# Five of thirteen weight slots moved by 32 bytes, and the down-projection tail of the second feed-forward moved from those five to the other eight

## The chip, the cores and the metric

The kernel runs on one core of a Trainium2 chip. The metric is the device time of one execution in microseconds (us); lower is better. The engines are named as the profile names them: PE is TensorE (matmuls), PEld its weight loads, DVE VectorE, ACT ScalarE, POOL GpSimd, SP the engine whose queue issues most DMAs.

## The reference, cut to what matters

Two layers over 256 tokens of width 1024, float32. A layer has two SwiGLU feed-forwards (inner width 2816), a mixer between them, and a gated embedding at its end; each ends in a layer norm of a scaled residual:

```python
for i in range(DEPTH):                       # DEPTH = 2
    x = layer_norm(ALPHA * x + 0.5 * swiglu(x, ffn1_w_up[i], ffn1_w_down[i]), ...)
    x = layer_norm(ALPHA * x + hybrid_mixer(x, ...), ...)
    x = layer_norm(ALPHA * x + 0.5 * swiglu(x, ffn2_w_up[i], ffn2_w_down[i]), ...)
    pe = p[i] @ ple_w_proj[i]
    x = layer_norm(ALPHA * x + sigmoid(x @ ple_w_gate[i] + ple_b_gate[i]) * pe, ...)
```

where `swiglu(x, up, down)` is `(silu(gate) * up) @ down`.

## The kernel before, in words

**Precision and passes.** Every large product is done in three passes of a rounded float32 type (fp32r): an operand v is split into v_hi (a copy, ACT, line 211 for weights, 300 for activations) and v_lo = v - v_hi (a subtraction, DVE, line 212 for weights, 291 for activations), and the passes are hi·hi, hi·lo and lo·hi. Activations stand in `XX` (hi and lo of all 1024 x 256 values) or, for a feed-forward chunk and for the embedding's input, in the pair `hh`, `hl` of 128 x 2 x 256 each.

**Two forms of matmul.** `mm_tok` (lines 329 to 331) keeps 128 x 128 of the activations in the array and streams the weights, 512 columns a matmul: 329 is hi·hi, 330 streams the weights' lo, 331 has the activations' lo in the array. `wide_feat` (364, 365, 367) and `mm_feat` (341 to 343) keep the weights in the array and stream activations.

**Weights.** 440 pieces of up to 128 x 1024 floats (512 KB), in one list in the order of use. Each is loaded by the SP queue into one of four raw buffers, then split into a slot: a pair of tiles `whi`, `wlo`. There are eight main slots for the whole kernel and five extra slots (`R_EXTRA`, line 33), which live in the pool `hp` of the feed-forward phases and are open to the pieces that `in_scope` (line 1158) admits. Pieces are loaded and split strictly in the list's order; the next piece goes into an extra slot if it is admitted and fewer than five are taken, else into a main slot if fewer than eight are taken, else it is not split yet (`room`, line 179). `in_scope` admits: of a feed-forward the down pieces of its last three chunks (8, 9, 10) and the up pieces of its first two; the output projection `wo`; and the embedding's `pe` and `pg`. A pool opened with the second feed-forward of a layer also serves that layer's embedding and the next layer's first feed-forward.

**When a piece is split.** This program's order is written by hand (`manual_schedule`): every engine runs its instructions in the order in which the code issues them. `W.free` (line 237) returns a slot and, unless `W.hold` is set, at once splits up to two next pieces. `W.hold` is set at line 555, after the first half of the tokens (t = 0, 128 tokens) has gone through the last three down chunks, so that DVE and ACT are left to the norm. From there a split comes where a table of marks puts one, after step i of a list of steps, one piece per `V`; `get` splits a piece on the spot if its user comes first and it is not there. The tables:

```python
GT = (6, 6)                # line 44: transposes of a norm's result after step 6
DT = (4, 4)
PT = (6, 6)
GA = " V V  VV"            # line 50: splits in the first chunks of layer 1's first feed-forward
DA = "  V V "              # line 51: in the down tail, t = 1
PA = "  V  VVV"            # line 54: in the embedding gate, t = 0
```

**The phases around the change.** (1) The tail of a feed-forward (`second`, then `steps(..., DT, turn0, DA)`): six down pieces, first with t = 0, then with t = 1, then the norm of t = 0 in between. (2) The embedding (`ple`, line 1026): hold is lifted, the products with `pe`, then eight gate steps with t = 0, one piece `pg` of 256 rows x 512 columns each (six matmuls, about 1.4 us a step); after step 3 the gate's first 512 columns are finished by a chain on DVE and ACT (`finish_cols`: lines 291, 1056, 294, 294, 399 for the norm's statistics); after step 6 TensorE transposes the t = 1 half of the norm before (`to_feat`, line 433) and ACT and DVE split the result into `XX` (lines 300, 291). (3) The first two chunks of the next layer's first feed-forward, eight steps with t = 0 of the same kind, marks `GA`.

A tile's name in the trace and in the order carries the piece: `wlo218` is the lo part of piece 218. In layer 0, 204 to 209 are the six down pieces of the second feed-forward's tail, 210 and 211 `pe`, 212 to 219 `pg` (four pairs), 220 to 227 the up pieces of the next first feed-forward's two first chunks. In layer 1 the same stand at 424 to 429, 430 to 431, 432 to 439, and nothing follows.

**Addresses.** Within a partition, modulo 256 bytes: `XX` lies at 128; the main slots, `hh` and `hl` and (before) the extra slots at 96.

Of the kernel before, what the change touches and what calls it, by code (L numbers as in the profile page):

```python
# [10 lines left out]
F32 = mybir.dt.float32  # L11
# [6 lines left out]
P = 128  # L18
# [4 lines left out]
NCH = FF // 256  # L23
# [6 lines left out]
LAG = 2  # L30
# [225 lines left out]
def build(tc, a, out):  # L256
# [12 lines left out]
    W = Weights(nc, a, rawp, wp)  # L269
    count = [0]  # L270

    def nm(s):
        count[0] += 1
        return f"{s}_{count[0]}"

    def ps():
        return psp.tile([P, 512], F32, tag="ps", name=nm("ps"))

    def work(n=512, dt=F32):
        return wk.tile([P, n], dt, tag="w", name=nm("w"))  # L280
# [6 lines left out]
    def load(dst, src):  # L287
        nc.sync.dma_start(dst, src)

    def tt(out, in0, in1, op):  # L290
        return V.tensor_tensor(out=out, in0=in0, in1=in1, op=op)  # L291

    def stt(out, in0, scalar, in1, op0, op1):
        return V.scalar_tensor_tensor(out=out, in0=in0, scalar=scalar, in1=in1, op0=op0, op1=op1)  # L294
# [9 lines left out]

    XX = const.tile([P, KD, 2, T], F32R, name="XX")
    XH, XL = XX[:, :, 0, :], XX[:, :, 1, :]
    XR = const.tile([P, 2, D], F32, name="XR")
# [11 lines left out]
    def mm_tok(o, t, w, k0, start, stop, lh=None, ll=None):  # L321

        lh, ll = (XH, XL) if lh is None else (lh, ll)
        hi, lo = w
        kt = hi.shape[1]
        c = slice(t * P, (t + 1) * P)
        for kk in range(kt):
            k = k0 + kk
            TE.matmul(o, lhsT=lh[:, k, c], rhs=hi[:, kk, :], start=start and kk == 0, stop=False)  # L329
            TE.matmul(o, lhsT=lh[:, k, c], rhs=lo[:, kk, :], start=False, stop=False)  # L330
            TE.matmul(o, lhsT=ll[:, k, c], rhs=hi[:, kk, :], start=False, stop=stop and kk == kt - 1)  # L331

    def mm_feat(o, w, col, k0=0, start=True, stop=True, rhs=None):

        rhs = XX if rhs is None else rhs
        hi, lo = w
# [16 lines left out]
    def wide_feat(key, free=True):  # L353
# [4 lines left out]
        for i in range(2):  # L358
            o = ps()
            hi, lo = W.get(key, i)  # L360
            for k in range(KD):
                both = XX[:, k].rearrange("p s c -> p (s c)")
                if k < KD - 1:
                    TE.matmul(o, lhsT=hi[:, k, :], rhs=both, start=k == 0, stop=False)  # L364
                TE.matmul(o[:, :T], lhsT=lo[:, k, :], rhs=XX[:, k, 0, :], start=False, stop=False)  # L365
                if k == KD - 1:
# [9 lines left out]
    def ln_params(l, i):  # L376
        tiles = []
        for j in range(2):
            t = gbp.tile([P, D], F32, tag="gb", name=nm("gb"))
            load(t, a["lnp"][(l * 4 + i) * 2 + j, :].partition_broadcast(P))  # L380
            tiles.append(t)
        return tiles
# [53 lines left out]
    def steps(work_list, at=(), turn=(), ahead="", inserts={}):  # L436

        for i, s in enumerate(work_list):
            s()
            for n, f in zip(at, turn):  # L440
                if n == i:
                    f()
            for f in inserts.get(i, ()):
                f()
            if ahead[i:i + 1] == "V":
                W.prefetch(1)


    def ffn(l, f, ln, hp, turn):
# [2 lines left out]
        d_keys = [(l, f, "d", c) for c in range(NCH)]  # L452

        def ht(c):
            hs[c] = [hp.tile([P, 2, T], F32R, tag=x, bufs=LAG + 2, name=nm(x)) for x in ("hh", "hl")]
            return hs[c]

# [11 lines left out]
        def first_chunk(key):  # L469

            o = [ps()[:, :T] for _ in range(4)]
            for k in range(KD):
                hi, lo = W.get(key + (k // 4,), k // 2 % 2)
                passes = [(x[:, k % 2, j * P:(j + 1) * P], XX[:, k, y, :], o[j], n) for n, (x, y) in enumerate(((hi, 0), (hi, 1), (lo, 0))) for j in range(4)]
                for w, x, oj, n in passes:
# [9 lines left out]

        if not first:
            ht(0), ht(1)

            def up_tok(t, c):
# [536 lines left out]
    def ple(l, turn, last):  # L1026
        pe = {}
        W.hold = False
        n_t = 0
        w = [W.get((l, "pe"), i) for i in range(2)]  # L1030

        def product(t, c0, m):
            o = ps()[:, :m]
            for i in range(2):
                mm_tok(o, t, [x[:, :, c0:c0 + m] for x in w[i]], i, i == 0, i == 1, *ple_in[l])
            return o

        def products(t, *blocks):
            for n, (c0, m) in enumerate(blocks):
                pe[t, n] = work()  # L1040
                S.activation(pe[t, n][:, :m], product(t, c0, m), AF.Copy)

        whole = (0, 512), (512, 512)

        products(0, *whole)
        bg = [work() for _ in range(2)]
        for n in range(2):
            load(bg[n], a["bg"][l, half[n]].partition_broadcast(P))
        gb = ln_params(l, 3)
        acc, norms = {}, {}  # L1050

        def finish_cols(t, n, o, c0, m, late=False):
            s = work(m)
            c = slice(c0 - 512 * n, c0 - 512 * n + m)
            tt(s, o, bg[n][:, c], ALU.add)
            S.activation(s, s, AF.Tanh, scale=0.5)
            stt(s, s, 1.0, product(t, c0, m) if late else pe[t, n][:, c], ALU.add, ALU.mult)
            norms[t].add(s, c0, m)
            norms[t].stats(c0, m)

        def step(t, n, h, i):
            if (t, n) not in acc:
                acc[t, n] = ps()
            key = (l, "pg", n, h)
            mm_tok(acc[t, n], t, W.get(key, i), 4 * h + 2 * i, h + i == 0, h + i == 2)
            if t == 1:
                W.free(key, i)
            if h + i == 2:
                if t not in norms:
                    norms[t] = Norm(t)  # L1070
                finish_cols(t, n, acc[t, n], 512 * n, 512)

        def last_step(q):

            o = ps()[:, :256]
            for h in range(2):
                for i in range(2):
                    key = (l, "pg", 1, h)
                    w = [x[:, :, q * 256:(q + 1) * 256] for x in W.get(key, i)]
                    mm_tok(o, 1, w, 4 * h + 2 * i, h + i == 0, h + i == 2)  # L1080
                    if q == 1:
                        W.free(key, i)
            finish_cols(1, 1, o, 512 + 256 * q, 256, q == 1)

        order = [(n, h, i) for n in range(2) for h in range(2) for i in range(2)]
        steps([lambda x=x: step(0, *x) for x in order], PT, turn, PA)
        products(1, *(((0, 512), (512, 256)) if last else whole))
        W.hold = True
        if not last:
            for i in range(2):  # L1090
                W.free((l, "pe"), i)
        turn0 = norms[0].finish(gb, last=last)
        if last:
            steps([lambda x=x: step(1, *x) for x in order[:4]] + [lambda q=q: last_step(q) for q in range(2)])
            return norms[1].finish(gb, ((0, 512), (512, 256), (768, 256)), True)
        steps([lambda x=x: step(1, *x) for x in order], QT, turn0, QA)
        return norms[1].finish(gb)
# [60 lines left out]
    def in_scope(i):  # L1158
        def allowed(key):
            l, name = key[:2]  # L1160
            if name in (1, 2):
                return (2 * l + name) // 2 == i and (key[2] == "d" and key[3] >= NCH - 1 - LAG or key[2] != "d" and key[3] < 2)
            return l + 1 == i and name in ("wo", "pe", "pg")

        return allowed

    def open_scope(i):
        sctx = ExitStack()
        hp = sctx.enter_context(tc.tile_pool(name=nm("ffn"), bufs=1, reuse_waits="tile"))
        W.open(hp, in_scope(i))  # L1170
        return sctx, hp

    sctx, hp = open_scope(0)
    turn = None
    for l in range(DEPTH):
        turn = ffn(l, 1, 0, hp, turn)
        W.close()
        sctx.close()
        gb, chains = mixer(l, turn)
        sctx, hp = open_scope(l + 1)  # L1180
        turn = merge_out(l, gb, chains)
        turn = ffn(l, 2, 2, hp, turn)
        turn = ple(l, turn, l == DEPTH - 1)
# [57 lines left out]
```

## Time and profile before

| | us |
|---|---|
| median of 3 runs (1295.80 to 1296.31) | 1296.01 |
| the profiled execution | 1296.62 |
| its span in the trace | 1294.8 |
| TensorE busy in the span | 1282.4 |
| DVE busy | 886.8 |
| ACT busy | 695.0 |

The span is the time between the first and the last instruction that the profile records on the core; the rest of the execution's time, 1.8 us, lies around it. Busy time is the union of an engine's instructions, so two matmuls that overlap in the array count once. The profile reads a wait as an idle stretch before an instruction, with the instruction that ended it in brackets behind an arrow.

### The profile page before, as it was taken

The page shows a single profiled execution, that of the slowest core. Times are in us where ns is not written, and L with a number is a line of the kernel's source. Part 1 is how long each engine was busy: PE and PEld are TensorE (multiplying, and loading weights), DVE is VectorE, ACT ScalarE, POOL GpSimd, SP SyncE. Part 2 cuts the span into 40 slices and gives each one's busy share as a digit, 9 for nine tenths or more (in the row PEclk, how much of TensorE's full clock was granted, in tenths as well). Part 3 has the DMA queues.
Part 4 walks back from the last instruction along what each step waited for, and adds up shares of the span by engine and source line. Part 5 has one row for each costly group of instructions (what it writes and reads, how often), then busy time and mean ns, then how long its engine had stood idle before and what let it go on. Part 6 is the DMA issues. An engine that isn't in the chain of part 4 may idle for free.

```text
span 1294.8 us, 20052 instructions
## 1 busy us (share of the span) xinstructions
PE 1282.4 (99%) x7934; PEld 1135.1 (88%) x7934; DVE 886.8 (68%) x1207; ACT 695.0 (54%) x1002; POOL 46.5 (4%) x42
## 2 busy tenths in 40 slices
PE   9999999999999999999999999999999999999997
PEld 8888888999999888888788888899999988888886
DVE  6767675687658666667876666765966586666686
ACT  6645544875455455555455455359654444545551
POOL 0000000000011000000000000000000110000000
PEclk9999999999999999999999999999999999999999
DMA  8775756455466465566565557374554655555651
GB/s 284 236 241 186 235 159 201 162 156 191 159 198 215 141 195 192 186 226 218 164 209 186 189 195 245 111 253 140 169 187 150 205 192 164 190 188 187 243 171 65
DMA packets 70061, 245.47 MB, mean 190 GB/s; under 512 B 8144, under 2 KB 8784, under 8 KB 69968
## 3 DMA queue, kind: packets, MB, share of 16 engines
q1 hardware_dynamic: 69680, 243.81, 57.3%
q8 instruction: 62, 1.02, 0.3%
q10 hardware_dynamic: 288, 0.39, 0.1%
q14 instruction: 31, 0.25, 0.1%
HBM read 243.12 MB, written 1.05 MB: 189 GB/s over the span
## 4 chain that ended last, share of the span: by engine, by line
PE 49%; DVE 1%; ACT 0%; issue 0%; DVEq 0%; ACTq 0%
PE ps L364 9%; PE ps L331 6%; PE ps L329 6%; PE ps L330 6%; PE ps L365 5%; PE ps L341 4%; PE ps L342 4%; PE ps L343 4%; PE ps L367 1%; PE ps L433 0%; DVE z L294 0%; PE ps L735 0%; DVE wlo L212 0%; PE ps L873 0%; PE ps L907 0%; PE ps L894 0%
## 5 line engine op out<-in xcount | busy, mean ns | idle before, releaser
L212 DVE TENSOR_TENSOR wlo<-raw,whi 128x1024 fp32r<-128x1024 f32 (+3 forms) x445 | 538.4, 1221 | 226.6 <-ACT whi L211 217.5
L211 ACT ACTIVATE whi<-raw 128x1024 fp32r<-128x1024 f32 (+3 forms) x445 | 458.3, 1039 | 200.5 <-PE ps L342 81.5
L364 PE MATMUL ps<-XX,whi 128*128 128x512 f32 x1036 | 368.3, 393 | 0.2 <-ACT w L481 0.2
L365 PE MATMUL ps<-XX,wlo 128*128 128x256 f32 x1184 | 308.3, 281 | 0.0
L365 PEld LDWEIGHTS ps<-XX,wlo 128*128 128x128 f32 x1184 | 223.0, 188 | 12.3
L364 PEld LDWEIGHTS ps<-XX,whi 128*128 128x128 f32 x1036 | 194.3, 188 | 40.1 <-ACT w L481 0.6
L341 PE MATMUL ps<-XX,whi 128*128 128x256 f32 x672 | 190.2, 283 | 0.0
L342 PE MATMUL ps<-XX,whi 128*128 128x256 f32 x672 | 187.7, 279 | 0.0
L343 PE MATMUL ps<-XX,wlo 128*128 128x256 f32 x672 | 187.6, 279 | 0.0
L329 PE MATMUL ps<-whi,hh 128*128 128x512 f32 (+1 forms) x370 | 144.8, 391 | 0.0
L331 PE MATMUL ps<-whi,hl 128*128 128x512 f32 (+1 forms) x370 | 144.0, 389 | 0.0
L330 PE MATMUL ps<-wlo,hh 128*128 128x512 f32 (+1 forms) x370 | 143.5, 388 | 0.0
L369 ACT ACTIVATE w<-ps 128x256 f32<-128x256 f32 x148 | 56.1, 382 | 156.0 <-PE ps L367 156.0
L329 PE MATMUL ps<-whi,XX 128*128 128x512 f32 (+2 forms) x360 | 138.8, 386 | 0.0
L331 PE MATMUL ps<-whi,XX 128*128 128x512 f32 (+2 forms) x360 | 137.1, 381 | 1.3 <-DVE XX L291 1.3
L330 PE MATMUL ps<-wlo,XX 128*128 128x512 f32 (+2 forms) x360 | 137.1, 381 | 0.0
L341 PEld LDWEIGHTS ps<-XX,whi 128*128 128x128 f32 x672 | 126.3, 188 | 1.6 <-issue 1.0
L342 PEld LDWEIGHTS ps<-XX,whi 128*128 128x128 f32 x672 | 126.4, 188 | 0.2
L343 PEld LDWEIGHTS ps<-XX,wlo 128*128 128x128 f32 x672 | 126.3, 188 | 0.0
L291 DVE TENSOR_TENSOR w<-ps,w 128x256 f32<-128x256 f32 (+1 forms) x157 | 67.9, 435 | 76.5 <-ACT w L369 75.0
L331 PEld LDWEIGHTS ps<-whi,hl 128*128 128x128 f32 x370 | 69.4, 188 | 15.3
L330 PEld LDWEIGHTS ps<-wlo,hh 128*128 128x128 f32 x370 | 69.5, 188 | 14.8
(178 smaller groups left out, 1384.6 us busy)
## 6 DMA issues: line engine op xcount, KB each, us to landing
raw<-in_wu SPq DMA_DIRECT2D x430, 512.0 KB, 4.1
gb<-in_lnp SPq DMA_DIRECT2D x16, 512.0 KB, 6.5
raw<-in_wu SPq DMA_DIRECT2D x8, 280.0 KB, 3.1
xr<-in_xT SPq DMA_DIRECT2D x4, 256.0 KB, 6.2
raw<-in_wu SPq DMA_DIRECT2D x4, 256.0 KB, 5.1
XR<-in_x SPq DMA_DIRECT2D x1, 1024.0 KB, 7.5
wa<-in_lru SPq DMA_DIRECT2D x2, 512.0 KB, 4.3
w<-in_bg SPq DMA_DIRECT2D x4, 256.0 KB, 4.4
```

Source lines behind the costliest of these rows:

```text
L211: self.nc.scalar.activation(hi[:, c], raw[:, c], AF.Copy)
L212: self.nc.vector.tensor_tensor(out=lw[:, c], in0=raw[:, c], in1=hi[:, c].bitcast(F32), op=ALU.subtract)
L291: return V.tensor_tensor(out=out, in0=in0, in1=in1, op=op)
L329: TE.matmul(o, lhsT=lh[:, k, c], rhs=hi[:, kk, :], start=start and kk == 0, stop=False)
L330: TE.matmul(o, lhsT=lh[:, k, c], rhs=lo[:, kk, :], start=False, stop=False)
L331: TE.matmul(o, lhsT=ll[:, k, c], rhs=hi[:, kk, :], start=False, stop=stop and kk == kt - 1)
L341: TE.matmul(o, lhsT=hi[:, kk, c], rhs=rhs[:, k, 0, :], start=start and kk == 0, stop=False)
L342: TE.matmul(o, lhsT=hi[:, kk, c], rhs=rhs[:, k, 1, :], start=False, stop=False)
L343: TE.matmul(o, lhsT=lo[:, kk, c], rhs=rhs[:, k, 0, :], start=False, stop=stop and kk == kt - 1)
L364: TE.matmul(o, lhsT=hi[:, k, :], rhs=both, start=k == 0, stop=False)
L365: TE.matmul(o[:, :T], lhsT=lo[:, k, :], rhs=XX[:, k, 0, :], start=False, stop=False)
L369: S.activation(lows[:, c], o[:, T:], AF.Copy)
```

## The change

It does four things. A tile of 8 floats (32 bytes) is put ahead of the extra slots in the pool `hp`, so that these lie 32 bytes further, at 128 modulo 256. A tile of 56 floats (224 bytes) ahead of `hh` and `hl` puts those back to 96. `in_scope` no longer admits the down pieces of a second feed-forward (`name == 1` is asked for), so they go to main slots; those of a first feed-forward stay in extra slots. And in the last layer `ple` returns the two slots of `pe` before its end.

```diff
--- before.py
+++ after.py
@@ -304,6 +304,8 @@
 
 
 
+
+
     XX = const.tile([P, KD, 2, T], F32R, name="XX")
     XH, XL = XX[:, :, 0, :], XX[:, :, 1, :]
     XR = const.tile([P, 2, D], F32, name="XR")
@@ -452,6 +454,8 @@
         d_keys = [(l, f, "d", c) for c in range(NCH)]
 
         def ht(c):
+            if c == 0:
+                hp.tile([P, 56], F32, tag="gap1", bufs=1, name=nm("gap"))
             hs[c] = [hp.tile([P, 2, T], F32R, tag=x, bufs=LAG + 2, name=nm(x)) for x in ("hh", "hl")]
             return hs[c]
 
@@ -1092,6 +1096,8 @@
         turn0 = norms[0].finish(gb, last=last)
         if last:
             steps([lambda x=x: step(1, *x) for x in order[:4]] + [lambda q=q: last_step(q) for q in range(2)])
+            for i in range(2):
+                W.free((l, "pe"), i)
             return norms[1].finish(gb, ((0, 512), (512, 256), (768, 256)), True)
         steps([lambda x=x: step(1, *x) for x in order], QT, turn0, QA)
         return norms[1].finish(gb)
@@ -1159,7 +1165,7 @@
         def allowed(key):
             l, name = key[:2]
             if name in (1, 2):
-                return (2 * l + name) // 2 == i and (key[2] == "d" and key[3] >= NCH - 1 - LAG or key[2] != "d" and key[3] < 2)
+                return (2 * l + name) // 2 == i and (key[2] == "d" and name == 1 and key[3] >= NCH - 1 - LAG or key[2] != "d" and key[3] < 2)
             return l + 1 == i and name in ("wo", "pe", "pg")
 
         return allowed
@@ -1167,6 +1173,7 @@
     def open_scope(i):
         sctx = ExitStack()
         hp = sctx.enter_context(tc.tile_pool(name=nm("ffn"), bufs=1, reuse_waits="tile"))
+        hp.tile([P, 8], F32, tag="gap0", name=nm("gap"))
         W.open(hp, in_scope(i))
         return sctx, hp
 
```

TensorE's instructions keep their order. What moves is which piece is split at which place on DVE and ACT, and with it the loads of SP. Up to the tail of the second feed-forward both kernels split the same pieces at the same places. When hold is set there, the kernel before has split 216 pieces (0 to 215): five of the six down pieces in the extra slots and 209 to 215 in main ones. The changed kernel has split 214: all six down pieces and two earlier ones in main slots, and 210 to 214 admitted to the five extra ones only. From there each mark splits a piece that comes two earlier in the list. (Names as above; line numbers of the changed kernel are two to four higher: its 401 is 399 of before, 435 is 433, 331 to 333 are 329 to 331.)

The first place is on DVE, in the embedding gate of layer 0, t = 0: the chain that finishes the first 512 columns, then the marks after steps 5 and 6. Before:

```order
L291 TENSOR_TENSOR w_449_6345<-ps_446_6312,w_442_6304 128x512
L294 SCALAR_TENSOR_TENSOR w_449_6345<-w_449_6345,w_438_6286 128x512
L294 SCALAR_TENSOR_TENSOR z_447_6343<-XR_82,w_449_6345 128x512
L399 BN_STATS s_448_6344<-z_447_6343 128x6
L212 TENSOR_TENSOR wlo220_6365<-raw220_6152,whi220_6364 128x1024
L291 TENSOR_TENSOR XX_81<-ps_451_6376,XX_81 128x4x128
L291 TENSOR_TENSOR XX_81<-ps_452_6383,XX_81 128x4x128
L212 TENSOR_TENSOR wlo221_6391<-raw221_6231,whi221_6390 128x1024
```

Now:

```order
L291 TENSOR_TENSOR w_453_6337<-ps_450_6304,w_446_6296 128x512
L294 SCALAR_TENSOR_TENSOR w_453_6337<-w_453_6337,w_442_6278 128x512
L294 SCALAR_TENSOR_TENSOR z_451_6335<-XR_82,w_453_6337 128x512
L401 BN_STATS s_452_6336<-z_451_6335 128x6
L212 TENSOR_TENSOR wlo218_6357<-raw218_6144,whi218_6356 128x1024
L291 TENSOR_TENSOR XX_81<-ps_455_6368,XX_81 128x4x128
L291 TENSOR_TENSOR XX_81<-ps_456_6375,XX_81 128x4x128
L212 TENSOR_TENSOR wlo219_6383<-raw219_6223,whi219_6382 128x1024
```

The two marks there split 218 and 219 in place of 220 and 221; the rest stands as it was. Steps 6 and 7 of the same list use 218 and 219. On TensorE this stretch reads as follows in the changed kernel (in the one before, the same rows with other tile numbers):

```order
L331 MATMUL ps_454_6343<-whi218_6356,XX_81 128x512
L332 MATMUL ps_454_6343<-wlo218_6357,XX_81 128x512
L333 MATMUL ps_454_6343<-whi218_6356,XX_81 128x512
L331 MATMUL ps_454_6343<-whi218_6356,XX_81 128x512
L332 MATMUL ps_454_6343<-wlo218_6357,XX_81 128x512
L333 MATMUL ps_454_6343<-whi218_6356,XX_81 128x512
L435 MATMUL ps_455_6368<-cf_83,XR_82 128x128 x4
L435 MATMUL ps_456_6375<-cf_83,XR_82 128x128 x4
L331 MATMUL ps_454_6343<-whi219_6382,XX_81 128x512
L332 MATMUL ps_454_6343<-wlo219_6383,XX_81 128x512
```

So step 6 stands right behind the split after step 5, and step 7 right behind the one after step 6, which on DVE itself stands behind both splits of the transposed half (the two rows into `XX`). The same holds for pieces 438 and 439 in layer 1; there the kernel before has nothing left to split at these marks, since 439 is the last piece.

The second place is on DVE in the first two chunks of layer 1's first feed-forward, t = 0: the end of the norm before and the marks of `GA`. Before:

```order
L212 TENSOR_TENSOR wlo226_6538<-raw226_6412,whi226_6537 128x1024
L406 BN_AGGR s_468_6543<-s_462_6473 128x2
L297 TENSOR_SCALAR s_469_6545<-s_468_6543 128x1
L294 SCALAR_TENSOR_TENSOR z_461_6472<-z_461_6472,s_468_6543,gb_444_6308 128x512 x2
L294 SCALAR_TENSOR_TENSOR XR_82<-z_461_6472,s_469_6545,gb_445_6310 128x512 x2
L212 TENSOR_TENSOR wlo227_6570<-raw227_6458,whi227_6569 128x1024
L291 TENSOR_TENSOR w_475_6587<-w_475_6587,ps_474_6556 128x256
L212 TENSOR_TENSOR wlo228_6591<-raw228_6484,whi228_6590 128x1024
L291 TENSOR_TENSOR XX_81<-ps_477_6615,XX_81 128x4x128
L291 TENSOR_TENSOR XX_81<-ps_478_6622,XX_81 128x4x128
L212 TENSOR_TENSOR wlo229_6630<-raw229_6503,whi229_6629 128x1024
```

Now:

```order
L212 TENSOR_TENSOR wlo224_6530<-raw224_6404,whi224_6529 128x1024
L408 BN_AGGR s_472_6535<-s_466_6465 128x2
L297 TENSOR_SCALAR s_473_6537<-s_472_6535 128x1
L294 SCALAR_TENSOR_TENSOR z_465_6464<-z_465_6464,s_472_6535,gb_448_6300 128x512 x2
L294 SCALAR_TENSOR_TENSOR XR_82<-z_465_6464,s_473_6537,gb_449_6302 128x512 x2
L212 TENSOR_TENSOR wlo225_6563<-raw225_6450,whi225_6562 128x1024
L291 TENSOR_TENSOR w_480_6580<-w_480_6580,ps_479_6549 128x256
L212 TENSOR_TENSOR wlo226_6584<-raw226_6476,whi226_6583 128x1024
L291 TENSOR_TENSOR XX_81<-ps_482_6608,XX_81 128x4x128
L291 TENSOR_TENSOR XX_81<-ps_483_6615,XX_81 128x4x128
L212 TENSOR_TENSOR wlo227_6623<-raw227_6495,whi227_6622 128x1024
```

Here the chunks' pieces 225, 226 and 227, which steps 5, 6 and 7 use, are split at the marks where before 227, 228 and 229 were.

## Rows read from the trace of the kernel before

**Rows 1.** the page: span, busy time by engine, and the granted clock in 40 slices.

```profile
span 1294.8 us, 20052 instructions
...
PE 1282.4 (99%) x7934; PEld 1135.1 (88%) x7934; DVE 886.8 (68%) x1207; ACT 695.0 (54%) x1002; POOL 46.5 (4%) x42
...
PEclk9999999999999999999999999999999999999999
```

**Rows 2.** groups by line and shape; busy us, mean ns of one, idle us.

```profile
L364 PE MATMUL ps<-XX,whi 128*128 128x512 f32 x1036 | 368.3, 393 | 0.2 <-ACT w L481 0.2
...
L330 PE MATMUL ps<-wlo,hh 128*128 128x512 f32 x366 | 142.4, 389 | 0.0
...
L330 PE MATMUL ps<-wlo,XX 128*128 128x512 f32 x312 | 123.3, 395 | 0.0
...
L1148 PE MATMUL ps<-cb 128*128 128x256 bf16 x20 | 4.4, 420 | 1.0 <-DVE cb L1145 1.0
```

**Rows 3.** timeline, first layer's embedding gate: start us, us, engine, instruction.

```profile
624.66 0.69 DVE L291 TENSOR_TENSOR w<-ps,w 128x512 f32<-128x512 f32 x1 [0.26 <-PE ps L331]
...
625.45 0.63 ACT L1056 ACTIVATE w<-w 128x512 f32<-128x512 f32 x1 [4.83 <-DVE w L291]
...
626.11 0.69 DVE L294 SCALAR_TENSOR_TENSOR w<-w,w 128x512 f32<-128x512 f32 x1 [0.76 <-ACT w L1056]
...
626.84 0.69 DVE L294 SCALAR_TENSOR_TENSOR z<-XR,w 128x512 f32<-128x512 f32 x1
...
627.50 0.40 PE L330 MATMUL ps<-wlo,XX 128*128 128x512 f32 x1
...
627.56 0.70 DVE L399 BATCH_NORM_STATS2 s<-z 128x6 f32<-128x512 f32 x1
...
628.17 1.21 DVE L212 TENSOR_TENSOR wlo<-raw,whi 128x1024 fp32r<-128x1024 f32 x1
...
628.66 1.03 PE L433 MATMUL ps<-cf,XR 128*128 128x128 f32 x8
629.30 1.09 ACT L300 ACTIVATE XX<-ps 128x512 fp32r<-128x512 f32 x2 [2.27 <-PE ps L433]
...
629.45 0.48 PE L329 MATMUL ps<-whi,XX 128*128 128x512 f32 x1
...
629.77 0.39 PE L330 MATMUL ps<-wlo,XX 128*128 128x512 f32 x1
...
630.27 1.06 ACT L211 ACTIVATE whi<-raw 128x1024 fp32r<-128x1024 f32 x1
...
630.70 0.39 PE L331 MATMUL ps<-whi,XX 128*128 128x512 f32 x1
...
631.36 1.23 DVE L212 TENSOR_TENSOR wlo<-raw,whi 128x1024 fp32r<-128x1024 f32 x1
...
632.51 0.68 DVE L291 TENSOR_TENSOR w<-ps,w 128x512 f32<-128x512 f32 x1
```

**Rows 4.** timeline, the same place of the second layer.

```profile
1268.68 0.40 PE L330 MATMUL ps<-wlo,XX 128*128 128x512 f32 x1
...
1268.75 0.70 DVE L399 BATCH_NORM_STATS2 s<-z 128x6 f32<-128x512 f32 x1
```

**Rows 5.** timeline, the one data wait of TensorE after the start.

```profile
646.94 1.28 DVE L291 TENSOR_TENSOR XX<-ps,XX 128x512 fp32r<-128x512 f32 x2
...
647.68 0.50 PE L331 MATMUL ps<-whi,XX 128*128 128x512 f32 x1 [1.30 <-DVE XX L291]
```

**Rows 6.** timeline, first two chunks of the second layer's first feed-forward.

```profile
654.55 0.40 PE L330 MATMUL ps<-wlo,XX 128*128 128x512 f32 x1
...
655.66 1.22 DVE L212 TENSOR_TENSOR wlo<-raw,whi 128x1024 fp32r<-128x1024 f32 x1
...
655.95 0.40 PE L330 MATMUL ps<-wlo,XX 128*128 128x512 f32 x1
...
657.13 1.22 DVE L212 TENSOR_TENSOR wlo<-raw,whi 128x1024 fp32r<-128x1024 f32 x1
```

## The prediction

> **What bounds the kernel now.** First the page: TensorE is busy for 1282.4 us of a span of 1294.8, and the granted clock reads 9 tenths or more in all 40 slices [rows 1]. So the kernel is bound by TensorE at its higher level (2.4 GHz), and only two things can change the time: how long matmuls take, and how long TensorE stands still. For the first I read the groups by line and shape [rows 2], for the second the timeline around the phases that the change moves. After the start-up TensorE has one data wait of over half a microsecond in the whole trace, 1.30 us for the transposed half in `XX`, in layer 1's first feed-forward [rows 5]. Everything else on DVE and ACT (886.8 and 695.0 us) is hidden; how far ahead of its use a split is finished decides whether it stays so.
>
> **The addresses.** The same matmul, lo weights streaming with 512 columns, has a mean of 389 ns where the activations in the array come from `hh`, and 395 where they come from `XX` [rows 2]. In the kernel before the first is the pair with equal addresses modulo 256 (96 and 96), the second the pair 32 bytes apart (96 and 128). I take these 6 ns for the offset's, though the rows could owe them to something else. The change brings pieces in extra slots in line with `XX`: of each layer's second feed-forward the 10 up pieces that stood in extra slots, layer 0's 5 of the next first feed-forward, and of the gate 3 in each layer, with twelve 512-column matmuls each over both halves of the tokens: 21 x 12 = 252 matmuls, counted over both layers (5 + 5 + 5 + 3 + 3 pieces). 252 x 6 ns = 1.5 us gained. It takes out of line what reads `hh` against an extra slot: the tail of both first feed-forwards (5 pieces each, 120 matmuls) and the `pe` products (42): 162 matmuls at 3 to 6 ns (393, the mean of the form with an offset of the other sign [rows 2], is about 4 over 389), say 5, lost: 0.8. The second feed-forward's tail stays in line, now in main slots. Net **-0.7**, between -1.9 (all gain at 7.5 ns, no loss) and 0 (no effect at all).
>
> On this the Trainium skill speaks against the change: "TensorE: Matmul & The Clock Gate", section "Step-by-step: what each phase is for", says that the array reads its streamed and its stationary operand through two independent ports, and that the next weights load beside the running matmul. By that rule two addresses have nothing to disturb each other with and this term is 0, the sum below 0.7 higher; the rows' 389 against 395 show that some difference exists, so I keep the term.
>
> **The splits.** The order shows that from the hold of layer 0's tail on each mark splits a piece two earlier in the list. TensorE's order is the same, so the pieces used next are split two marks later than they were. Where this leaves a piece finished before TensorE wants it, it costs nothing (the down tail and the first steps of the gate, where a piece was two to four steps ahead). It does not in these places:
>
> *Place A, the embedding gate, t = 0.* The DVE chain of the gate's first half starts at 624.66 when step 3's last matmul ends, goes over ACT and two more DVE instructions to the statistics at 627.56, and only then does the mark's subtraction run, 628.17 for 1.21 us [rows 3]. In the changed kernel that is piece 218, done at 629.38; TensorE wants it for its second matmul of step 6, which stood at 627.50 [rows 3]. **1.9** us. Then the rest shifts with TensorE: the transposes, at 628.66, ACT's two copies into `XX` at 629.30 (1.09), then ACT's copy of the next weights at 630.27 for 1.06, then DVE's subtraction at 631.36 for 1.23, behind its own two splits of the transposes. These are now piece 219, which step 7 wants at 629.45 (hi) and 629.77 (lo) [rows 3]. Hi is 630.27 + 1.06 - 629.45 = 1.9 late, lo 631.36 + 1.23 - 629.77 = **2.8**, of which the 1.9 are part. Place A costs 1.9 + 2.8 = 4.7.
>
> In layer 1 the kernel before has no split here; the change adds it (438, 439). The statistics begin at 1268.75 and TensorE's matmul stands at 1268.68 [rows 4]: 1268.75 + 0.70 + 1.21 (a split's row) is 1270.66, less 1268.68 gives 2.0; the statistics' row overlaps the next by 0.1 in layer 0, so again 1.9. The second part is the same sequence: 4.7. Both layers: **+9.4**.
>
> *The old wait.* TensorE is 4.7 late behind place A of layer 0. DVE's next chain, at 632.51 [rows 3], waits for step 7's last matmul: 630.70 + 0.39 + 4.7 = 635.8, so DVE is 3.3 late. It has gained 1.4 on TensorE, and the wait of 1.30 at 647.68, for DVE's split at 646.94 [rows 5], goes: **-1.3**. Behind it TensorE is 3.4 late.
>
> *Place B, layer 1's first chunks, t = 0.* Step 5 wants the lo of 225 where 654.55 stands, now 654.55 + 3.4 = 657.95; the mark's subtraction stood at 655.66 for 1.22 [rows 6], now 3.3 later: 660.2. **2.2** us. Step 6 wants 226 at 655.95 + 3.4 + 2.2 = 661.55; DVE has it at 657.13 + 1.22 + 3.3 = 661.65: 0.1. Piece 227 is split behind the transposes, as 219 is: 2.8 by place A's rows. Place B costs **+5.1**, if DVE is as late as I say: it runs the end of a norm there and has no idle time to catch up in.
>
> *Smaller edits.* After a wait the first matmul runs longer (0.50 at 647.68 [rows 5] against 0.39 to 0.40): 0.1 each over some ten waits, of which I take half, +0.5. Loads come up to two pieces earlier or later in the SP queue; raw buffers stay four, a load is issued when a raw buffer is returned by its split, long ahead of the splits here: 0. If that cover failed, a late load would add to a wait that is there already. Returning `pe` in the last layer, when the pieces that may use it are all split or admitted already, costs no instruction: 0. The gap tiles have no instruction either.
>
> Sum: 9.4 - 1.3 + 5.1 - 0.7 + 0.5 = **+13.0** against the profiled execution's 1296.62 (span 1294.8 [rows 1] and 1.8 around it), 1309.6. That execution is 0.6 above the median of 1296.01, so the forecast for the median is **1309.0**.
>
> **The rivals.** 0.2%, about what can be told from no change, is 2.6 us.
>
> *Place B is absorbed.* If DVE's work behind place A waits less for TensorE than I hold, DVE gains more than 1.4 and place B's 5.1 shrink towards nothing: 1309.0 - 5.1 = 1303.9. For it: DVE is busy for two thirds only. Against: in that stretch DVE is what TensorE already waits for [rows 5].
>
> *The clock falls.* TensorE stands for 2 to 3 us several times within 10 us, which it does nowhere in the trace after the start. The start shows the price: 20 matmuls of 256 columns took 4.4 us there [rows 2], 220 ns each, the lower level of 1.2 GHz, while at place A six matmuls of 512 columns go from 627.50 to 628.66 [rows 3], some 230 ns each, the higher. A stretch as long as the start's at half pace loses 2.2 us. At all three places: 1309.0 + 6.6 = 1315.6. The same page of the Trainium skill, section "Why this matters for your kernels", warns of idle gaps in the middle of a kernel, since the clock falls behind them. The rows cannot confirm it: behind the 1.30 of [rows 5] the clock holds, and a longer stop is not there.
>
> *No slower: the splits stay hidden.* One mechanism decides place A's first part and by its kin the rest: from the end of step 3 to the mark's subtraction DVE takes 628.17 + 1.21 - 624.66 = 4.7 us, and TensorE reaches the matmul that wants it after 2.8. If in the changed kernel the subtraction is not held behind that chain, because DVE takes it up before step 3 ends, within those 2.8, all waits vanish, and only the addresses' -0.7 and perhaps the -1.3 are left: 1295.3 or 1294.0. For it: DVE often idles before the chain. Against: each engine keeps its order, and the order has the subtraction behind the chain. The same time comes out if the change does not do what it says, that is, if pieces do not come two later; the order excludes that.
>
> **How the numbers follow.** The forecast has 0.78: it is arithmetic on rows in a fixed order. Place B absorbed 0.08, the clock 0.08, no slower 0.06. The range reaches down to place B absorbed with the addresses at their full -1.9: 1303.9 - 1.2 = 1302.7; up to no address effect (+0.7), restarts twice as dear (+0.5) and the clock lost at one of the places (+2.2): 1309.0 + 3.4 = 1312.4. It leaves out the clock at all places and the last rival. Faster by over 0.2%: 0.02, part of the last rival with both gains (1294.0 is 2.0 below, so only if the addresses give more); within 0.2%: 0.04; slower: 0.94.
>
> **What the new profile would show.** Right: TensorE waits of about 1.9 and then twice of a sum of 2.8 (for ACT's hi, then DVE's lo), for `wlo218` and `whi219`, `wlo219`, again for 438 and 439, and for 225 to 227 in between; none for `XX` at the old place; TensorE's busy time without the waits less by about 0.7; `XX` rows of line 330 split into more at 389. Wrong: waits at other tiles, fewer than nine of them, a clock digit under 9 around half or at the end of the span, or a busy time that rises.

## The result, and the profile after

| | before | after |
|---|---|---|
| median, us (5 runs each) | 1296.01 | 1317.17 |
| lowest to highest | 1295.51 to 1296.59 | 1315.80 to 1318.23 |
| profiled execution, us | 1296.62 | 1316.03 |
| its span | 1294.8 | 1314.3 |

The ratio is 1.0163, interval [1.0152, 1.0174]: 21 us slower. The forecast was 13.0 slower with a range that ended at 1312.4; the direction holds, the size does not, and the time lies outside the range. The page of the changed kernel, as in [rows 1]:

```profile
span 1314.3 us, 20047 instructions
...
PE 1290.5 (98%) x7934; PEld 1139.9 (87%) x7934; DVE 888.1 (68%) x1207; ACT 695.1 (53%) x1002; POOL 46.5 (4%) x42
...
PEclk9999999999999999999999999999999999999998
```

TensorE runs the same 7934 matmuls and is busy for 8.1 us longer. Had only waits been added, its busy time would hardly have moved: here the matmuls themselves became slower somewhere. A busy time that rises and a clock digit under 9 at the end of the span are two of the signs by which the prediction was to be known as wrong, and both are there. The digits show little more: a slice of 1/40 of the span is 33 us long, and the last one reads 8 also in a kernel without any of the losses below (the last experiment's). First the waits of TensorE, all of the trace (what waited, for whom, us in total, times, the longest):

```profile
PE ps L332 <- DVE wlo L212: 8.1, 6, 2.3
PE ps L331 <- ACT whi L211: 5.1, 3, 1.7
PE ps L1154 <- DVE cb L1151: 1.0, 1, 1.0
PE ps L480 <- ACT whi L211: 0.8, 1, 0.8
PE ps L366 <- ACT w L485: 0.3, 1, 0.3
```

The first two lines are new, 13.2 us in nine waits for split weights; the last three belong to the start. The wait for `XX` of [rows 5] is gone. Place A of layer 0 in the timeline (start, duration, engine, instruction; idle time before it and what ended it in brackets), to be laid beside [rows 3]:

```profile
627.24 0.40 PE L331 MATMUL ps<-whi,XX 128*128 128x512 f32 x1
627.54 0.69 DVE L401 BATCH_NORM_STATS2 s<-z 128x6 f32<-128x512 f32 x1
628.15 1.21 DVE L212 TENSOR_TENSOR wlo<-raw,whi 128x1024 fp32r<-128x1024 f32 x1
...
629.42 0.50 PE L332 MATMUL ps<-wlo,XX 128*128 128x512 f32 x1 [1.78 <-DVE wlo L212]
...
631.33 1.08 ACT L300 ACTIVATE XX<-ps 128x512 fp32r<-128x512 f32 x2 [4.32 <-PE ps L435]
...
632.29 1.06 ACT L211 ACTIVATE whi<-raw 128x1024 fp32r<-128x1024 f32 x1
633.38 1.23 DVE L212 TENSOR_TENSOR wlo<-raw,whi 128x1024 fp32r<-128x1024 f32 x1
...
633.41 0.50 PE L331 MATMUL ps<-whi,XX 128*128 128x512 f32 x1 [1.68 <-ACT whi L211]
...
634.67 0.80 PE L332 MATMUL ps<-wlo,XX 128*128 128x512 f32 x1 [0.76 <-DVE wlo L212]
...
635.26 0.63 PE L333 MATMUL ps<-whi,XX 128*128 128x512 f32 x1
...
635.69 0.63 PE L331 MATMUL ps<-whi,XX 128*128 128x512 f32 x1
...
636.11 0.63 PE L332 MATMUL ps<-wlo,XX 128*128 128x512 f32 x1
```

The three waits are where the arithmetic put them: the lo of 218 behind the statistics, the hi of 219 behind ACT's copies of the transposed half, its lo behind DVE's. But behind the third, matmuls take 0.63 us instead of 0.40 and follow one another after 0.43 (635.26, 635.69, 636.11) instead of 0.23. That is half pace. Stretches of 2 us at the three places, with the granted clock as the third figure from the right (the figures ahead: us, then busy time and count of TensorE, its weight loads, DVE, ACT, POOL; behind it DMA share and GB/s):

```profile
632.00:634.00 2.00, 0.50 (x1) 0.19 (x1) 1.86 (x3) 1.35 (x2) 0.00 (x0) 1.00 0.04 14
634.00:636.00 2.00, 1.33 (x3) 1.14 (x4) 0.61 (x1) 0.00 (x0) 0.00 (x0) 0.67 0.23 35
636.00:638.00 2.00, 2.00 (x6) 1.52 (x6) 0.69 (x1) 0.07 (x1) 0.00 (x0) 0.50 0.61 227
660.00:662.00 2.00, 0.27 (x1) 0.27 (x2) 2.00 (x4) 0.00 (x0) 0.00 (x0) 1.00 0.10 41
662.00:664.00 2.00, 2.00 (x6) 1.54 (x6) 1.14 (x2) 0.00 (x0) 0.00 (x0) 0.50 0.62 186
664.00:666.00 2.00, 2.00 (x8) 1.53 (x7) 0.00 (x0) 0.00 (x0) 0.00 (x0) 0.65 0.83 281
1282.00:1284.00 2.00, 1.59 (x5) 1.21 (x6) 0.36 (x1) 0.00 (x0) 0.00 (x0) 0.81 0.00 0
1284.00:1286.00 2.00, 1.96 (x9) 1.50 (x7) 0.23 (x1) 0.60 (x2) 0.00 (x0) 0.50 0.00 0
1286.00:1288.00 2.00, 0.41 (x1) 0.19 (x1) 1.59 (x3) 1.53 (x2) 0.00 (x0) 0.84 0.00 0
1288.00:1290.00 2.00, 1.24 (x6) 0.98 (x6) 0.79 (x1) 0.00 (x0) 0.00 (x0) 1.00 0.00 0
1290.00:1292.00 2.00, 2.00 (x7) 1.56 (x6) 0.92 (x2) 0.63 (x1) 0.00 (x0) 0.51 0.00 0
1292.00:1294.00 2.00, 2.00 (x11) 1.77 (x10) 1.90 (x4) 0.60 (x1) 0.00 (x0) 0.63 0.04 8
```

Four stretches at the lower level, 1.2 GHz: one at place A of layer 0, one at place B, two at place A of layer 1. What a stretch lost is the missing share times its 2 us, summed: 1.7 at the first (0.33 and 0.50, and 0.03 just behind the last row), 1.7 at the second, and 3.4 at the last two together, of which some 0.3 (the share missing from 1286 to 1288) fell in idle time. Some 6.5 us in all by this estimate.

The sum for the profiled execution's 19.4 us is best taken from the start of one matmul to the start of the next, since neighbours overlap, and laid beside the same matmuls of the trace before. The nine waits come to 15.0, more than the 13.2 that is shown as idle, because a matmul behind a wait cannot overlap the one ahead of it (627.24 to 629.42 is 2.18 where 0.23 is usual: 1.95, and 1.78 of it is shown as idle). The matmuls of the slow stretches come to 6.0. The old wait takes off 1.5, and everything else, the addresses included, 0.1. Together 19.4.

### The profile page after: what moved, and what is told of

The parts are those of the page before. It is cut to its first block, busy times and chain, and to the rows that moved or that the text cites. A ratio compares the mean times of both kernels' runs of the same rounds, so it can differ in the third digit from the quotient of the medians.

```text
span 1314.3 us, 20047 instructions
## 1 busy us (share of the span) xinstructions
PE 1290.5 (98%) x7934; PEld 1139.9 (87%) x7934; DVE 888.1 (68%) x1207; ACT 695.1 (53%) x1002; POOL 46.5 (4%) x42
## 4 chain that ended last, share of the span: by engine, by line
PE 48%; DVE 2%; ACT 0%; issue 0%; DVEq 0%; ACTq 0%
PE ps L366 9%; PE ps L332 6%; PE ps L333 6%; PE ps L331 6%; PE ps L367 5%; PE ps L343 4%; PE ps L344 4%; PE ps L345 4%; PE ps L369 1%; DVE wlo L212 1%; PE ps L435 0%; DVE z L294 0%; DVE w L294 0%; PE ps L739 0%; ACT w L1060 0%
## 5 line engine op out<-in xcount | busy, mean ns | idle before, releaser
L332 PEld LDWEIGHTS ps<-wlo,XX 128*128 128x128 f32 x360 | 68.3, 190 | 23.3 <-DVE wlo L212 10.2
L331 PEld LDWEIGHTS ps<-whi,XX 128*128 128x128 f32 x360 | 68.2, 189 | 19.2 <-ACT whi L211 5.9
```

## The experiments

Times are medians; the ratio is to the kernel before on the same chip, whose median was 1295.7 to 1296.0 in the three series. Each experiment names the kernel that it edits.

**Offset alone.** The changed kernel with the old rule of `in_scope` and without the return of `pe`:

```diff
-  ... (key[2] == "d" and name == 1 and key[3] >= NCH - 1 - LAG or ...
+  ... (key[2] == "d" and key[3] >= NCH - 1 - LAG or ...
```

> Only the 32 bytes (both gap tiles); the second feed-forward's down tail stays in the extra slots, so pieces are split where they were before. Theory (waits plus a fallen clock): none of the new waits, the old wait of 1.3 us stays; 234 matmuls of 512 columns come in line with XX, 240 of both tails go out of line with hh and hl, 6 ns each either way: 0.0, so 1296.0 +- 0.5. Rival (the offset itself slows the extra slots' matmuls, and that is what the forecast lacked): some 8 us slower, 1304.

Measured: 1296.48, ratio 1.0004 [0.9995, 1.0013]. The offset alone does nothing that can be told, and TensorE's one late wait is the old one again. Its groups of the streamed lo weights:

```profile
L332 PE MATMUL ps<-wlo,hh 128*128 128x512 f32 x366 | 142.9, 390 | 0.0
...
L332 PE MATMUL ps<-wlo,XX 128*128 128x512 f32 x312 | 122.9, 394 | 0.0
```

389 and 395 of [rows 2] moved towards each other by one each, as about a quarter of each group changed sides: the gain and the loss are both there, and cancel. Matmul by matmul against the trace before, most of those whose weights moved take 4 to 6 ns less against `XX` and as much more against `hh` and `hl`, and the others change by nothing. Neither `XX` nor `hh` moved, and the same shift of the slots helps against one and hurts against the other, so for weights that stream it is the distance between the two operands that counts.

**The other slots alone.** The changed kernel without its two gap tiles.

> Only the other slots for the down tail (and the return of pe's slots); no gap tile, extra slots at 96 as before. Theory: all the waits and the low clock of the changed kernel, without the addresses' gain of about 0.8: 1318.0, within 1.5 of the changed kernel. Rival (the offset costs the 8 us): 1309, the forecast's waits alone.

Measured: 1317.80, ratio 1.0165 [1.0151, 1.0179], clock 0.991 in its profile against 0.998 before; 12.7 us of waits for split weights. All of the loss, the slower clock included, comes with the moved splits. The 0.6 above the changed kernel is less than the runs scatter.

**Matmuls in the waits.** The changed kernel with TensorE kept busy while it waits; the fills write PSUM tiles that the next user overwrites, so the results stay what they are:

```diff
+FILL = (16, 25, 18, 25)
+    def fill(n):
+        o = ps()
+        spare.append(o)
+        for _ in range(n):
+            TE.matmul(o[:, :256], lhsT=ident16, rhs=flat(cb16), start=True, stop=True)
...
+            if t == 0 and n == h == 1:
+                fill(FILL[i])
             mm_tok(acc[t, n], t, W.get(key, i), 4 * h + 2 * i, h + i == 0, h + i == 2)
```

> The changed kernel with matmuls put into the new waits: 16 and 25 bf16 matmuls of 256 columns ahead of steps 6 and 7 of the embedding gate (both layers), 18 and 25 ahead of steps 5 and 7 of layer 1's second chunk, their results overwritten unused. At 109 ns each they take 1.7 and 2.7, 2.0 and 2.7 us, less than the waits, so they delay nothing and only keep TensorE busy. Theory: the clock stays at its higher level, the splits are as late as before, so the time is the forecast's 1309 +- 1 with TensorE granted clock back at 0.998. Rival (the missing 8 us are not the clock's): 1317, as the changed kernel.

Measured: 1309.88 (1309.56 to 1310.90), ratio 1.0106 [1.0092, 1.0120]. 7.3 us come back although no split is earlier. The mean clock of its profile, and place A in stretches:

```profile
core 0: 1308.1 us, clock 0.998
```

```profile
628.00:630.00 2.00, 1.99 (x12) 1.38 (x10) 0.64 (x1) 0.00 (x0) 0.00 (x0) 1.00 0.31 78
630.00:632.00 2.00, 2.00 (x20) 1.88 (x19) 0.77 (x2) 1.40 (x3) 0.00 (x0) 1.00 0.54 213
632.00:634.00 2.00, 2.00 (x18) 1.55 (x16) 1.75 (x2) 0.63 (x1) 0.00 (x0) 1.00 0.00 0
```

(Over the whole stretch from 10 to 1300 us it reads 1.00.) The changed kernel's mean is 0.993. Behind each fill the next matmul with a lo part still starts 0.05 to 0.06 us after that part's subtraction ends, so the fills delay nothing and the splits are as late as before. This separates the two costs: the late splits are worth 14 us (1309.9 against 1296.0), idleness itself another 7, through the clock.

**Half of the fills.** The same with the first wait of each place filled, `FILL = (16, 0, 18, 0)`, and with the second, `(0, 25, 0, 25)`.

> As the kernel with filled waits, but only the first wait of each place is filled (16 matmuls ahead of step 6, 18 ahead of step 5 of the chunk); the second, 1.8 us for hi and 1.0 for lo with one matmul between, stays idle. If it is this longer one that lets the clock fall: three stretches at the lower level of 2.2 us lost each, 1309.9 + 6.6 = 1316.5. If it takes both waits together: 1310.

> The other half: only the second wait of each place is filled (25 matmuls ahead of step 7); the first, 1.9 us (2.4 in layer 1's second chunk), stays idle. If a wait of 2 us suffices for the clock to fall: up to 1316.5, as above. If only the longer second one does it: 1310, or 1312 with the 2.4 us one falling.

Measured: 1311.16, ratio 1.0118 [1.0104, 1.0132], and 1311.71, ratio 1.0122 [1.0108, 1.0136]. The 1316.5 named as an upper end for both does not come; each profile has just one stretch at the lower level. 1311.71 is near the 1312 that was expected if only the longest single wait, at place B, lets the clock fall, but the fall came at another place. First wait filled (the fall is in place B), then second wait filled (the fall is in layer 1's place A):

```profile
664.00:666.00 2.00, 0.26 (x3) 0.12 (x1) 1.42 (x3) 1.83 (x3) 0.00 (x0) 1.00 0.45 176
666.00:668.00 2.00, 1.24 (x4) 0.79 (x5) 1.09 (x1) 0.00 (x0) 0.00 (x0) 0.89 0.00 0
668.00:670.00 2.00, 2.00 (x7) 1.51 (x6) 0.24 (x1) 0.65 (x2) 0.00 (x0) 0.50 0.78 262
```

```profile
1278.00:1280.00 2.00, 1.26 (x5) 1.02 (x6) 0.68 (x1) 0.00 (x0) 0.00 (x0) 0.88 0.00 0
1280.00:1282.00 2.00, 2.00 (x10) 1.80 (x9) 0.00 (x0) 0.50 (x1) 0.00 (x0) 0.50 0.00 0
```

A single wait lets the clock fall at one place and not at another where it is just as long (the first wait of layer 0's place A is as long as layer 1's, and the clock held behind it here and in the changed kernel); with both left idle it falls at every place. It need not be the place that decides: in the profile of the kernel with the other slots alone, the same first wait of layer 0's place A, 1.77 us up to 628.28, has the fall right behind it, and a second one follows behind the second wait:

```profile
628.00:630.00 2.00, 1.72 (x5) 1.39 (x6) 0.23 (x1) 0.00 (x0) 0.00 (x0) 0.65 0.40 123
630.00:632.00 2.00, 2.00 (x10) 1.62 (x8) 0.00 (x0) 0.59 (x1) 0.00 (x0) 0.50 0.38 145
...
636.00:638.00 2.00, 2.00 (x7) 1.52 (x6) 0.66 (x1) 0.00 (x0) 0.00 (x0) 0.50 0.69 262
```

So behind waits of the same length at the same place the clock falls in one execution and holds in another. What decides is not settled.

**Two more marks.** The changed kernel with

```diff
-DA = "  V V "
+DA = " VVVV "
```

> The changed kernel with DA = ' VVVV ' for '  V V ': two more pieces are split in the second feed-forward's tail (and the first's), so that the marks behind it split the pieces they did before the change. Theory (all of the loss is pieces split two late, and what hangs on that): the nine waits go, the old one of 1.3 comes back, and only the addresses' gain of 0.9 is left: 1295.1. Rival (DVE has no room for two more splits beside the norm in the tail): new waits of TensorE at the transposes behind the tail, 1297 to 1301.

Measured: 1295.45, ratio 0.9995 [0.9986, 1.0004]. Behind the start, TensorE's old wait alone is left:

```profile
PE ps L333 <- DVE XX L291: 1.4, 1, 1.4
...
PE ps L480 <- ACT whi L211: 0.5, 2, 0.3
```

So the tail has room on DVE for two more splits, and the whole loss hung on the lead of two pieces. **One more mark**, `DA = " VV V "`:

> The changed kernel with one mark more in the tail, DA = ' VV V ', so that pieces are split one late instead of two. Theory: place A's splits come one mark earlier, behind step 2 and 5 for what steps 5 and 6 use, and have a whole step in hand: no wait there; in layer 1's first chunks piece 226 is split where 227 was in the kernel before and is about 1.2 late. No clock loss from so short a wait: 1295.4 + 1.2 = 1296.6. Rival (the price grows with each piece): half of the loss, 1306.

Measured: 1297.07, ratio 1.0009 [1.0000, 1.0018], with one new wait, of 1.0 (start to start 1.1), where it was expected:

```profile
PE ps L332 <- DVE wlo L212: 1.0, 1, 1.0
```

The price is no slope: one piece late costs 1 to 2 us more than none (1297.07 against 1295.45, from two series), two cost 22.

**The addresses by themselves.** Three kernels move only `XX` in the kernel before, by a tile ahead of it and one behind it that together make 256 bytes: first level with the slots (224 bytes ahead), then 64 (32 bytes ahead) and 128 (96) off them:

```diff
+    const.tile([P, 56], F32, name="gapx")
     XX = const.tile([P, KD, 2, T], F32R, name="XX")
+    const.tile([P, 8], F32, name="gapy")
```

> The kernel before with another edit: 224 bytes ahead of XX and 32 behind it, so that XX lies at 96 modulo 256 as the weight slots, hh and hl do; nothing else moves, no piece is split elsewhere. If equal addresses are worth 6 ns wherever weights stream against XX: 936 matmuls x 6 = 5.6 less. The 1036 matmuls that stream XX against weights in the array come in line too; 28 of them did in the changed kernel and took 234 ns from start to start against 231, 3 ns more each, which by that would cost 3.1. Together 1293.5; without the second 1290.4. Rival (the addresses are no cause, the forms differ by something else): 1296.0.

> The kernel before with XX at 160 modulo 256, 64 bytes off the weight slots, in place of 128; nothing else moves. If only an offset of 32 bytes or only equal addresses matter can be read from each form. Theory (streaming weights is fast only at equal addresses; streaming XX is slow only there): no form changes, 1296.0. Rival (32 bytes is the disturbed offset of the streamed weights): 936 x 6 ns less, 1290.4. Third: another offset has a price of its own, more than 1297.

> The kernel before with XX at 224 modulo 256, 128 bytes off the weight slots. Same theories as for 64 bytes: 1296.0; or 1290.4; or more than 1297.

Measured: 1299.67, ratio 1.0028 [1.0017, 1.0040]; 1297.60, ratio 1.0015 [1.0006, 1.0024]; 1301.32, ratio 1.0040 [1.0027, 1.0054]. The first misses every expected value, the other two are the third case, more than 1297. The groups of the first (level):

```profile
L366 PE MATMUL ps<-XX,whi 128*128 128x512 f32 x1036 | 371.8, 398 | 0.2 <-ACT w L483 0.2
...
L343 PE MATMUL ps<-XX,whi 128*128 128x256 f32 x672 | 193.0, 287 | 0.0
...
L332 PE MATMUL ps<-wlo,XX 128*128 128x512 f32 x312 | 121.7, 390 | 0.0
```

of the second (64 off):

```profile
L366 PE MATMUL ps<-XX,whi 128*128 128x512 f32 x1036 | 370.4, 395 | 0.4 <-ACT w L483 0.4
...
L343 PE MATMUL ps<-XX,whi 128*128 128x256 f32 x672 | 190.1, 283 | 0.0
```

and of the last (128 off):

```profile
L366 PE MATMUL ps<-XX,whi 128*128 128x512 f32 x1036 | 370.7, 394 | 0.5 <-ACT w L483 0.5
...
L343 PE MATMUL ps<-XX,whi 128*128 128x256 f32 x672 | 191.9, 286 | 0.0
...
L332 PE MATMUL ps<-wlo,XX 128*128 128x512 f32 x312 | 123.1, 395 | 0.0
```

Before, `XX` streamed with 512 columns took 393, the streamed weights 395 [rows 2], and the 256-column form

```profile
L341 PE MATMUL ps<-XX,whi 128*128 128x256 f32 x672 | 190.2, 283 | 0.0
```

Level addresses do speed up the weights that stream against `XX`, from 395 to 390, and slow down `XX` streaming against weights by 5 (512 columns) and 4 (256 columns, a form that my expectation had left out: 672 each at three lines). 64 or 128 off changes nothing for the streamed weights (395); the 512-column form of `XX` takes 1 to 2 ns more than before at both, the 256-column form 2 to 3 more at 128 and none at 64. So each form has its own order of the four distances tried. A mean in these rows is a duration, and neighbours overlap; the price is what the starts say. From start to start, level against before, the streamed weights come to -5.4 us, the streaming `XX` to +4.5 with 512 columns and to +6.0 in the three 256-column lines (341 to 343 of before) and -1.0 in a fourth (365): with small change +4.0, which is what the two profiled executions differ by (1300.64 and 1296.62). The addresses are a cause. For `XX` streaming, no run parts the distance from `XX`'s own place, and that 256 bytes is the period was taken and not tested.

**A version that beats both.** On the changed kernel:

```diff
-DA = "  V V "
-PA = "  V  VVV"
-QA = " V V V V"
+DA = " VVVV "
+PA = " VVV VVV"
+QA = " V V  VV"
...
-  ... == i and (key[2] == "d" and name == 1 and key[3] >= NCH - 1 - LAG or key[2] != "d" and key[3] < 2)
+  ... == i and key[2] != "d" and key[3] < 2
```

> The changed kernel with two marks more in the tail (DA = ' VVVV '), the marks of the embedding gate moved forward (PA = ' VVV VVV', QA = ' V V  VV'), and the first feed-forward's down tail, too, in main slots. Theory: no wait of the changed kernel is left; the old one of 1.4 us shrinks by some 1.1, since DVE has a split less between the gate and the transposes it is late for; 120 matmuls of the first feed-forwards' tails are back in line, 0.6: 1295.45 - 1.1 - 0.6 = 1293.7, 2.3 below the kernel before. Rival (the mixer's first pieces then come two late, as the gate's did): 1296 or more.

Measured: 1293.94, ratio 0.9985 [0.9977, 0.9994]: 1.8 us under the kernel before, small but clear of its interval.

```profile
PE ps L480 <- ACT whi L211: 0.7, 1, 0.7
PE ps L333 <- DVE XX L291: 0.2, 1, 0.2
```

The old wait is down to 0.2. No run parts the 1.8; from start to start in the two traces the wait gives some 1.1 and the addresses 0.5.

## Why the prediction was right or wrong

*The splits: right.* Nine waits at the tiles named, none elsewhere. Against the forecast's 1.9, 1.9 and 2.8 in all, place A shows 1.78, 1.68 and 1.68 + 0.76 idle, in layer 1 1.77, 1.63 and 1.63 + 0.76; place B 2.25 for 2.2, none for 0.1, and 1.74 + 0.76. Counted from start to start they are 15.0 where the forecast had 14.5 and 0.5 for restarts. With the clock held, the filled kernel came to 1309.88 where the forecast said 1309.0.

*The old wait: right.* It is gone after the change and back with the two more marks (1.4).

*The addresses: right for one matmul, too large in the sum.* In line the streamed matmul takes 390 against 395 in the level kernel, as the prediction took it to. Of its 252 matmuls gained and 162 lost, the changed kernel with two more marks shows some 190 and 150, worth -1.2 and +1.0 from start to start and together -0.3, where -0.7 stood in the sum. Its median is 0.5 under the kernel before, which its interval does not tell from nothing. From the Trainium skill's two independent read ports ("TensorE: Matmul & The Clock Gate", "Step-by-step: what each phase is for") the prediction drew the rule that addresses have nothing to disturb, which the page itself does not say. The level kernel contradicts the rule: an edit of addresses alone moved 936 matmuls by -5 ns and 3052 others by +4 to +5, and the time by 3.8 us.

*Place B absorbed, and no slower: wrong as rivals.* DVE was as late as the rows said; the order kept the subtraction behind the chain.

*The clock: the step that failed.* The prediction's words were: "The rows cannot confirm it: behind the 1.30 of [rows 5] the clock holds, and a longer stop is not there." From that it gave the fall a chance of 0.08, left it out of the sum, and let the range take it at one place only (+2.2), though its own sum put waits of 1.9 and 2.8 us, ten microseconds apart at most, where the trace had no example. One wait of 1.3 is no evidence on two longer ones. What the runs showed in its place is a clock that fell behind every one of the three places, four stretches and 6.0 us in all, and that held, with 7.3 us given back, once the waits were filled. The rival's 1315.6 came near by luck: it had three falls of 2.2 us, the profile has four of some 1.7, and the 2.2 is half of the time that the start's matmuls took, which says nothing on how long a fall lasts. (A slip beside it changes nothing: from 627.50 to 628.66 there are five matmuls and not six, 232 ns each.) So the arithmetic stood ready and the weight was on the wrong case: the forecast itself created the condition, and the rows could not support a chance as small as 0.08. The Trainium skill's page named above ("TensorE: Matmul & The Clock Gate") says in "Why this matters for your kernels" to leave no idle gaps in the middle of a kernel, and has longer single gaps in mind than any here. The trace bears out the advice and goes beyond the limit: 0.50 was granted behind every one of the three places though no wait of that trace was longer than 2.25 us, and the mean is 0.998 once the gaps are filled.

## What to carry to other kernels

A change of the slots that pieces may take also changes how far ahead they are prepared: count the pieces done at each mark, before and after, since one piece less can cost 1 to 2 us and two can cost 20. Where a forecast adds idle time to TensorE in the middle of a busy kernel, price the slower clock behind it as part of the forecast, not as a rival; filling the gap with matmuls tells the two costs apart. Where operands lie is worth some 3 to 6 ns of a matmul here (of 230 with 512 columns, from start to start), with opposite signs for opposite roles, so it has to be measured for each form.

## What was not expected of the hardware

The matmul's time depends on where its operands lie, in the four distances tried modulo 256 bytes: weights streaming, 390 ns level against 395 at 32, 64 or 128 bytes apart; `XX` streaming, 398 level, 393 at 32, 395 at 64, 394 at 128. And the same pair of waits cost one stretch at the lower clock level in layer 0 and two in layer 1: the fall came behind the second part at place A of layer 0, behind the first at place B, behind each in layer 1. That is one execution. With the same nine waits, the profile of the kernel with the other slots alone has two stretches at place A of layer 0, one at place B, and at layer 1's place A the lower level without a break from 1284 to 1294 us. So the number of falls differs between executions with the same waits. The mean clock of the changed kernel's five runs, 0.991 to 0.993, is in keeping with that, and their times scatter by 2.4 us where those before scatter by 1.1; how much of that scatter is the clock's is not shown.
